# A hybrid decoder layer on one core: the mixer's input weights split early, stored in DRAM and read back as pairs

## The chip, the cores and the metric

The kernel runs on one core of a Trainium2 chip. The metric is the device time of one execution in microseconds (us): 1100.04 us is the median of 3 runs before the change (1100.03 to 1100.62). The engines are called as in the profile: PE (TensorE matmuls; PEld its weight loads), DVE (VectorE), ACT (ScalarE), POOL (GpSimd) and SP (SyncE, which here issues nearly all DMAs, in one queue).

## What is computed

One layer on 512 tokens of width 1024, in three sub-layers, each followed by a layer norm:

```python
mod = silu(c) @ w_ada + b_ada                 # 9 vectors of 1024: shifts, scales, gates
h = swiglu_ffn(modulate(x, sh1, sc1), w1, w3, w2);  x = layer_norm(ALPHA * x + 0.5 * g1 * h)
h = hybrid_mixer(modulate(x, sh2, sc2), w_in, ...); x = layer_norm(ALPHA * x + g2 * h)
h = swiglu_ffn(modulate(x, sh3, sc3), w1', w3', w2'); x = layer_norm(ALPHA * x + 0.5 * g3 * h)
```

The mixer multiplies its input by `w_in` (1024 x 3280), and from the columns come a sparse attention (index scores, top-k by repeated maximum, softmax over the kept keys) and a gated delta rule (short convolutions, a triangular inverse per chunk, a recurrence over four chunks). Both go through `w_out`.

## The kernel before, in words

**Split products.** Matmuls in fp32 are made of three matmuls in the faster fp32r type: every operand is split into a high part (a rounded copy, made by ACT) and a low part (the rest, made by a subtraction), and `mm3` issues high*high, high*low and low*high into one PSUM bank. A weight tile of 128 x 1024 takes one `wload` into a `raw` buffer, and `weights` turns it into `wh` and `wl` tiles, 512 columns at a time: `wh` by ACT, `wl` by DVE, or by POOL where the call says `pool=True`. There are 5 raw buffers (NRAW) and 86 tiles of 128 x 512 (NBIG), of which the weights' parts may hold a quota (`wf` 32, `wm` 16, `wb` and `w2` 28).

**Stages.** The first feed-forward network runs first: a first group of four hidden tiles (`first_group`, PSUM tiles `g`), then 18 steps f with 48 matmuls each (tiles `p`), then the down-projection in ten pieces (tiles `y`). In it, `ada` computes the modulation: 72 chunks of `w_ada`, each a load into a raw buffer and one multiply-and-sum on DVE (`raw<-raw,silu_c`); 16 stand ahead of the first matmuls, 2 follow each step f and 3 each piece of the down-projection until all are done.

The mixer's step `first` makes two key and value tiles and four index-query tiles from `wina` (8 blocks of 128 x 768, loaded into `wb` tiles and split by ACT and POOL). The other 20 column tiles come from `winb`: `project` loads one 128 x 1024 tile, splits it with ACT and POOL, and multiplies it in 24 matmuls (tiles `pj`). Steps `pk`, `pq`, `pv` convolve them, `qa` makes attention queries, `z` gates. `ix`, `tk`, `lg`, `av` are index scores, top-k, softmax weights and values (tiles `pt`, `pv`). `pre` and `sub` prepare and invert the triangular blocks: `sub` takes two raw buffers (`bl`, `Y`) and runs 31 pairs of a product and a subtraction on DVE, and then `m64`, `m128`, `rec` (one after the other over the four chunks) and `out` follow; they are the tail of the mixer, ahead of most of the output projection (tiles `y`), which again is split by ACT and DVE. The second network is built as the first.

**What sets the order.** Every operation is recorded first (so nearly all rows of the profile have line 561, that of the emitting loop), and a planner puts them in order: each has a priority by its place in the program, a table `ORDER` gives the mixer's steps and their delays, and the planner plays its own model of the engines, the buffers and the quotas. The result is a fixed order on every engine and in SP's queue. On the chip each engine keeps to it and waits at semaphores.

Of the kernel before, what the change touches and what calls it, by code (L numbers as in the profile page):

```python
# [11 lines left out]
F32 = mybir.dt.float32  # L12
F32R = mybir.dt.float32r
# [4 lines left out]
P = 128  # L18
T = 512
D = 1024  # L20
KD = D // P
# [5 lines left out]
NBIG, NRAW, WF, WM, WB, W2 = 86, 5, 32, 16, 28, 28  # L27
SKEW, DEFER = 3, 500
ALPHA = 2.0 ** 0.25
LN_EPS = 1e-5  # L30
# [534 lines left out]
class Build:  # L565
# [54 lines left out]
    def weights(s, src, n, pool=False, big=False):  # L620
# [22 lines left out]
        return get  # L643

    def mm3(s, out, wh, wl, xh, xl, start, stop):
        mm = s.nc.tensor.matmul
        mm(out, wh, xh, start=start, stop=False)
        mm(out, wh, xl, start=False, stop=False)
        mm(out, wl, xh, start=False, stop=stop)

    def setup(s):
        nc = s.nc
        s.par = s.keep(NPAR, "par")
        s.cst = s.keep(NCST, "cst")
        s.sc = s.keep(D, "silu_c")
        s.g.strict = True
        nc.sync.dma_start(s.sc, s.d["c"].broadcast_to([P, D]))
        nc.scalar.activation(s.sc, s.sc, AF.Silu)
        s.mod = {v: s.keep(8, f"mod_{v}") for v in range(9)}
        s.ada_next = 0  # L660
        s.early = [s.wload(s.d["wada"][j], D) for j in range(2)]
        nc.sync.dma_start(s.par, s.d["par"])
        zero, pb = s.t("zero")[:, 0:P], s.bank("warm")[:, 0:P]
        nc.gpsimd.memset(zero, 0.0)
        for _ in range(WARM):
            nc.tensor.matmul(pb, zero, zero, start=True, stop=True)
# [19 lines left out]
    def ada_some(s, n):  # L686
        for _ in range(n):
            if s.ada_next < len(ADA_CHUNKS):
                s.ada()

    def glu(s, p1, p3):
        nc = s.nc
# [4 lines left out]

    def first_group(s, src, us, halves, big=False):


        nb = src.shape[2] // P
        banks = [s.bank("g") for _ in range(nb)]
# [3 lines left out]
        def go(k, c0, c1):  # L706
            uh, ul = us(k, c0, c1)
            if k not in ws:
                q, s.quota = s.quota, "w2" if s.quota == "wm" else "wb"
                ws[k] = s.weights(src[k], nb * P, pool=True, big=True)  # L710
                s.quota = q
# [13 lines left out]
    def ffn(s, n, us, halves, ada_plan, res):  # L725
# [11 lines left out]
        for f in range(NF - G0[n]):  # L737
# [6 lines left out]
            hs.append(s.glu(p1, p3))  # L744
            s.ada_some(ada_plan(f))
        ws = {}
        for dt, c0, c1 in pieces(2):
# [9 lines left out]
            if c1 == T:  # L757
                del ws[dt]
            s.ada_some(ada_plan(100 + dt))

# [82 lines left out]
def body(s):  # L843
# [31 lines left out]

    s.ffn(1, us1, ALL, lambda f: 2 if f < 100 else 3, res1)

# [97 lines left out]

    s.ffn(2, u3, HALF, lambda f: 0, res3)
    fin = ln_apply(s.p_("ln3g"), s.p_("ln3b"), None, None, need_u=False)
# [86 lines left out]
def project(s, us, i, n=2):  # L1064

    res = []
    for b in range(n):
        w = s.weights(s.d["winb"][i + b], 1024, pool=True)
        pb = s.bank("pj")
# [121 lines left out]
def attend_values(s, ps, v2, qt, g, att):  # L1191
# [18 lines left out]
    for j in range(2):  # L1210
# [5 lines left out]

ORDER = ("first qi0 qa0:5766 ks:51 pk1:451 spill:57 pk3:1103 pq1:8 z2 qi1:17 gt:131 ix1 pv2:684 pq2:3860 pk2:1987 "
# [5 lines left out]

# [16 lines left out]
class Mixer:  # L1240
# [25 lines left out]
    def first(s):  # L1266

        b, nc = s.b, s.nc
        banks = b.first_group(b.d["wina"], s.us, HALF)
        b.quota = "wm"  # L1270
# [169 lines left out]
    def sub(s):  # L1440
# [3 lines left out]
        bl, Y = (b.g.tile(b.wraw, [P, B * B], F32, "raw", b.name(t), NRAW)[:n] for t in ("bl", "Y"))  # L1444
        tmp = b.sc[:n]
        for c in range(4):
# [167 lines left out]
```

## Time and profile before

| | |
|---|---|
| median of 3 runs | 1100.04 us |
| the profiled execution | 1099.98 us, span 1098.2 us |
| PE busy | 1061.3 us (97%) |
| DVE busy | 679.3 us (62%) |
| ACT busy | 414.9 us (38%) |
| POOL busy | 302.3 us (28%) |
| moved by DMA | 137.92 MB, mean 126 GB/s |

The span is what the profile covers; the execution's own time is 1.8 us longer. PE's busy time is a modelled one: matmuls overlap, so that a busy PE need not run at its peak, and a lower granted clock makes the same matmuls busy for longer. Shares over the span are means over very different stages; the rows ahead of the prediction are therefore by stage.

### The profile page before, as it was taken

To read this page: it belongs to the slowest core of one execution; us is meant where nothing else is said; L and a number is where in the kernel's file an instruction comes from. 1 tells how busy PE (TensorE), PEld (TensorE's weight loads), DVE (VectorE), ACT (ScalarE), POOL (GpSimd) and SP (SyncE) were. 2 spreads that over 40 slices of the span, in tenths; PEclk is the share of its full clock that TensorE was granted. 3 is DMA by queue.
4 is the path that set the end of the run, shared out by engine and by line. 5 is a ranking of instruction groups with operands and counts; after the bars stand their busy time and mean duration, and the time that the engine had idled before them with its cause. 6 is when DMAs were issued, how large, how long until landed. Compare 5 with 4: busy or idle time off the path is not lost.

```text
span 1098.2 us, 15160 instructions
## 1 busy us (share of the span) xinstructions
PE 1061.3 (97%) x5520; PEld 904.5 (82%) x5520; DVE 679.3 (62%) x1506; ACT 414.9 (38%) x866; POOL 302.3 (28%) x308
## 2 busy tenths in 40 slices
PE   8999999999999989999969999999999999999996
PEld 6788888888888988787747898989888888888896
DVE  7997655547672466999988999884333323333314
ACT  3353323233231434765832566443333322322203
POOL 4600000000222695496824311695000000002210
PEclk9999999999999999998959999999999999999998
DMA  9878555547642412131112303611323222243002
GB/s 359 314 278 316 206 179 196 172 138 244 221 156 91 137 54 98 40 109 46 44 43 52 103 21 125 235 45 41 113 83 110 92 81 72 68 144 106 16 1 77
DMA packets 52203, 137.92 MB, mean 126 GB/s; under 512 B 11360, under 2 KB 15584, under 8 KB 52128
## 3 DMA queue, kind: packets, MB, share of 16 engines
q1 hardware_dynamic: 52048, 136.69, 37.4%
q8 instruction: 43, 0.70, 0.3%
q14 instruction: 32, 0.26, 0.1%
q0 software_dynamic: 80, 0.26, 0.1%
HBM read 131.17 MB, written 5.77 MB: 125 GB/s over the span
## 4 chain that ended last, share of the span: by engine, by line
PE 75%; DVE 15%; issue 3%; ACT 3%; POOL 3%; DMA 1%; SPq 0%; POOLq 0%; ACTq 0%; DVEq 0%
PE p L561 37%; PE y L561 26%; PE g L561 6%; DVE sc L561 2%; DVE raw L561 2%; POOL wl L561 2%; DVE m L561 1%; PE pv L561 1%; DVE cv L561 1%; DVE x L561 1%; PE pj L561 1%; DVE u L561 1%; DVE Y L561 1%; PE pt L561 1%; DVE ptl L561 1%
## 5 line engine op out<-in xcount | busy, mean ns | idle before, releaser
L561 DVE TENSOR_TENSOR wl<-raw,wh 128x512 fp32r<-128x512 f32 (+1 forms) x260 | 180.1, 709 | 151.8 <-ACT wh L561 79.5
L561 ACT ACTIVATE wh<-raw 128x512 fp32r<-128x512 f32 (+1 forms) x300 | 174.7, 615 | 186.1 <-PE y L561 82.4
L561 PE MATMUL p<-ul,wh 128*128 128x512 f32 x592 | 230.3, 389 | 0.0
L561 PE MATMUL p<-uh,wh 128*128 128x512 f32 x592 | 230.3, 389 | 0.0
L561 PE MATMUL p<-uh,wl 128*128 128x512 f32 x592 | 230.3, 389 | 0.0
L561 PE MATMUL y<-hh,wl 128*128 128x512 f32 (+1 forms) x440 | 152.9, 347 | 0.0
L561 PE MATMUL y<-hl,wh 128*128 128x512 f32 (+1 forms) x440 | 152.7, 347 | 0.0
L561 PE MATMUL y<-hh,wh 128*128 128x512 f32 (+1 forms) x440 | 152.5, 347 | 0.0
L561 DVE CUSTOM_DVE_ANT_0 raw<-raw,silu_c 128x1024 f32<-128x1024 f32 x72 | 96.8, 1354 | 75.5 <-DMA raw<-in_wada_dram 75.5
L561 POOL TENSOR_SCALAR s<-x 128x512 f32<-128x512 f32 x3 | 4.0, 1332 | 461.4 <-DVE x L561 461.4
L561 PEld LDWEIGHTS p<-ul,wh 128*128 128x128 f32 x592 | 111.2, 188 | 23.2
L561 PEld LDWEIGHTS p<-uh,wl 128*128 128x128 f32 x592 | 111.1, 188 | 22.9
L561 PEld LDWEIGHTS p<-uh,wh 128*128 128x128 f32 x592 | 111.2, 188 | 22.8
L561 PEld LDWEIGHTS y<-hh,wh 128*128 128x128 f32 x440 | 83.3, 189 | 10.4
L561 PEld LDWEIGHTS y<-hl,wh 128*128 128x128 f32 x440 | 83.3, 189 | 10.4
L561 PEld LDWEIGHTS y<-hh,wl 128*128 128x128 f32 x440 | 83.3, 189 | 10.2
L561 ACT ACTIVATE hh<-sil 128x512 fp32r<-128x512 f32 x44 | 27.7, 633 | 154.9 <-DVE sil L561 135.0
L561 PE MATMUL g<-ul,wh 128*128 128x256 f32 (+1 forms) x256 | 78.8, 319 | 1.7 <-DVE ul L561 1.6
L561 PE MATMUL g<-uh,wh 128*128 128x256 f32 (+1 forms) x256 | 66.4, 316 | 9.9 <-ACT uh L561 9.9
L561 PE MATMUL g<-uh,wl 128*128 128x256 f32 (+1 forms) x256 | 75.5, 316 | 0.0
L561 POOL TENSOR_TENSOR wl<-wb,wh 128x512 fp32r<-128x512 f32 (+1 forms) x48 | 61.1, 1295 | 22.6 <-DMA wb<-in_f1a_dram 18.1
L561 POOL TENSOR_TENSOR s<-s,x 128x512 f32<-128x512 f32 (+1 forms) x21 | 28.5, 1356 | 137.0 <-DVE x L561 126.0
(254 smaller groups left out, 1826.8 us busy)
## 6 DMA issues: line engine op xcount, KB each, us to landing
raw<-in_wada_dram SPq DMA_DIRECT2D x72, 512.0 KB
raw<-in_f2b_dram SPq DMA_DIRECT2D x38, 512.0 KB
raw<-in_f1b_dram SPq DMA_DIRECT2D x36, 512.0 KB
raw<-in_winb_dram SPq DMA_DIRECT2D x20, 512.0 KB
raw<-in_f1c_dram SPq DMA_DIRECT2D x16, 512.0 KB
raw<-in_f2c_dram SPq DMA_DIRECT2D x16, 512.0 KB
wb<-in_f1a_dram SPq DMA_DIRECT2D x16, 256.0 KB
raw<-in_wout_dram SPq DMA_DIRECT2D x8, 512.0 KB
```

The source lines that it names most:

```text
L561: getattr(getattr(s.nc, o.eng), o.meth)(*[real(x) for x in o.args], **{k: real(v) for k, v in o.kw.items()})
```

## The change

A new step, `presplit`, runs beside the first network: once behind each of the 18 steps f and twice behind each piece of the down-projection, until the 8 tiles of `wina` and the 20 of `winb` are done. It loads a tile into a raw buffer, ACT writes the high part into a second raw buffer, DVE puts the low part in the place of the tile, and two DMAs write both to DRAM tensors (`dwa`, `dwb`). In the mixer, `stored` takes the place of `weights`: it reads the two parts back, those of `wina` into 512-column tiles (`wd`), those of `winb` into two raw buffers, from which the matmuls read. No engine splits these weights in the mixer. The modulation's chunks get other places: 3 behind each of the first four pieces only, and the last 8 behind the steps of the second network. `sub` takes a tile of its own for its products (`tmp`) in place of the buffer of silu(c), which is needed longer. The table `ORDER` is another one.

```diff
+    def presplit(s):
+        nc = s.nc
+        if s.pre_next >= KD + 20:
+            return
+        i, s.pre_next = s.pre_next, s.pre_next + 1
+        n, src = (768, s.d["wina"][i]) if i < KD else (1024, s.d["winb"][i - KD])
+        dst = s.dwa[i] if i < KD else s.dwb[i - KD]
+        raw = s.wload(src, n)
+        hi = s.g.tile(s.wraw, [P, 1024], F32, "raw", s.name("rawh"), NRAW)
+        nc.scalar.activation(hi[:, :n].bitcast(F32R), raw[:, :n], AF.Copy)
+        nc.vector.tensor_sub(raw[:, :n].bitcast(F32R), raw[:, :n], hi[:, :n])
+        nc.sync.dma_start(dst[0], hi[:, :n])
+        nc.sync.dma_start(dst[1], raw[:, :n])
+
+    def stored(s, src, n, big=False):
...
+            else:
+                x = s.g.tile(s.wraw, [P, 1024], F32, "raw", s.name("wd"), NRAW)
+                nc.sync.dma_start(x[:, :n], src[j])
+                parts.append([x[:, o:o + 512] for o in range(0, n, 512)])
...
+    def plan(s, f):
+        s.ada_some(2 if f < 100 else 3 if f < 104 else 0)
+        for _ in range(PRE_F if f < 100 else PRE_D):
+            s.presplit()
...
-    s.ffn(1, us1, ALL, lambda f: 2 if f < 100 else 3, res1)
+    s.ffn(1, us1, ALL, s.plan, res1)
-    s.ffn(2, u3, HALF, lambda f: 0, res3)
+    s.ffn(2, u3, HALF, lambda f: s.ada_some(1), res3)
-        w = s.weights(s.d["winb"][i + b], 1024, pool=True)
+        w = s.stored(s.dwb[i + b], 1024)
-        banks = b.first_group(b.d["wina"], s.us, HALF)
+        banks = b.first_group(b.dwa, s.us, HALF, nb=6)
-ORDER = ("first qi0 qa0:5766 ks:51 pk1:451 spill:57 pk3:1103 pq1:8 z2 qi1:17 gt:131 ix1 pv2:684 pq2:3860 pk2:1987 "
+ORDER = ("first qi0:239 ks:38 qa0:3221 pk2:3522 pv2:686 gt:451 pq2:815 z2:82 qi1:275 pk3:561 ix2 ix3:175 ix1 pk1 "
-        tmp = b.sc[:n]
+        tmp = b.t("tmp")[:n]
```

The first place is SP's queue beside the steps f of the first network. Before, two tiles of `f1b` (the network's own weights) and two of `wada` take turns:

```order
L561 DMA raw_1096<-in_f1b_dram 128x1024
L561 DMA raw_1119<-in_f1b_dram 128x1024
L561 DMA raw_1134<-in_wada_dram 128x1024
L561 DMA raw_1170<-in_wada_dram 128x1024
L561 DMA raw_1175<-in_f1b_dram 128x1024
L561 DMA raw_1205<-in_f1b_dram 128x1024
L561 DMA raw_1219<-in_wada_dram 128x1024
```

In the change, beside a later step:

```order
L562 DMA raw_1243<-in_winb_dram 128x1024
L562 DMA raw_1257<-in_f1b_dram 128x1024
L562 DMA raw_1272<-in_f1b_dram 128x1024
L562 DMA raw_1277<-in_wada_dram 128x1024
L562 DMA dwb<-rawh_1275 128x1024
L562 DMA dwb<-raw_1243 128x1024
L562 DMA raw_1319<-in_wada_dram 128x1024
L562 DMA raw_1334<-in_winb_dram 128x1024
```

A load of `winb` and two stores have come between the loads of each step, and the stores wait in the queue for ACT and DVE.

The second place is PE's order in the recurrence, between the second chunk's new state (`Sn`, `o`) and the products of the third chunk with it (`kS`, `qS`). Before, some fifty rows of attention stand between the two, of which these are the first:

```order
L561 MATMUL Sn_6105<-dl_6090,ktok_4604 128x128 x4
L561 MATMUL o_6115<-dl_6090,aq_5233 128x128 x4
L561 MATMUL pv_6124<-pth_6099,vh_4824 128x256
L561 MATMUL pv_6124<-ptl_6111,vh_4824 128x256
L561 MATMUL pv_6124<-pth_6099,vl_4835 128x256
L561 MATMUL pv_6124<-pth_6099,vh_4854 128x256
L561 MATMUL pv_6124<-ptl_6111,vh_4854 128x256
```

In the change:

```order
L562 MATMUL Sn_6429<-dl_6417,ktok_4605 128x128 x4
L562 MATMUL o_6439<-dl_6417,aq_5241 128x128 x4
L562 MATMUL y_1334_6448<-X_6272,y_1333_6431 128x128 x4
L562 MATMUL kS_6457<-S_6441,cv_4255 128x128
L562 MATMUL kS_6457<-S_6441,cv_4142 128x128
L562 MATMUL kS_6457<-S_6441,cv_4428 128x128
```

The attention work has left this stretch: between the first product of `m64` and the last transpose of `out`, 48 of 56 `pt`, 77 of 89 `pv` and all 32 `lg` matmuls now stand ahead of it.

The third place is DVE's order within `sub` (in the change its products go to `tmp`). Rope and query rows (`rq`, `rp`, `qs`) of the last attention queries, which before stood behind `sub`, now stand between its pairs:

```order
L562 TENSOR_TENSOR rp_5733<-rp_5733,sw_5730 128x512
L562 TENSOR_TENSOR Y_5100<-Y_5100,tmp_5558 64x15x17
L562 TENSOR_TENSOR atl_5394<-pv_5563,ath_5384 128x128
L562 TENSOR_TENSOR tmp_5558<-bl_5278,Y_5100 64x252
L562 TENSOR_TENSOR qs_5755<-rp_5733,qs_5755 64x512
L562 TENSOR_TENSOR Y_5100<-Y_5100,tmp_5558 64x14x18
L562 TENSOR_TENSOR qs_5761<-rp_5733,qs_5761 64x512
```

In all, DVE has 324 rows between the last `ul` ahead of the mixer and the first pair of `sub` (282 before), 132 from there to its last pair (103 before) and 222 (294 before) from there to the next norm's `ul`.

## Rows read from the trace of the kernel before

**Rows 1.** Windows by stage: window, then busy us (instructions) by engine, PEclk, DMA, GB/s

```profile
52.00:258.00 206.00, 206.00 (x909) 170.62 (x910) 135.66 (x258) 69.51 (x126) 0.43 (x1) 1.00 0.62 209
258.00:381.00 123.00, 123.00 (x676) 107.63 (x675) 65.40 (x134) 33.76 (x63) 34.92 (x31) 1.00 0.51 165
381.00:395.00 14.00, 11.58 (x96) 11.18 (x95) 10.17 (x22) 8.51 (x20) 12.93 (x14) 1.00 0.34 114
425.00:560.00 135.00, 126.56 (x593) 101.67 (x591) 126.70 (x329) 90.83 (x209) 89.62 (x89) 0.93 0.19 61
560.00:597.00 37.00, 31.56 (x134) 25.54 (x134) 32.96 (x104) 11.47 (x31) 9.48 (x12) 0.78 0.00 1
597.00:676.00 79.00, 77.56 (x570) 70.35 (x568) 70.65 (x258) 45.05 (x133) 18.46 (x23) 1.00 0.28 84
395.00:676.00 281.00, 265.23 (x1510) 225.56 (x1510) 244.79 (x714) 150.90 (x380) 143.48 (x158) 0.93 0.20 64
730.00:1098.00 368.00, 359.38 (x1821) 307.56 (x1820) 132.55 (x232) 108.59 (x195) 44.40 (x50) 0.99 0.24 75
```

**Rows 2.** The chain that ended last, first network: start us, us, what

```profile
62.06 195.84 PE p L561 x864
```

**Rows 3.** Groups of POOL, 381 to 700 us: busy us, mean ns, then idle before

```profile
L561 POOL TENSOR_TENSOR wl<-raw,wh 128x512 fp32r<-128x512 f32 x36 | 48.4, 1360 | 28.7 <-ACT wh L561 20.8 <-PE pj L561 7.9
L561 POOL TENSOR_TENSOR wl<-wb,wh 128x512 fp32r<-128x512 f32 (+1 forms) x14 | 14.7, 1077 | 1.0 <-ACT wh L561 0.9
```

**Rows 4.** Groups of DVE by form, 395 to 676 us

```profile
L561 DVE TENSOR_TENSOR qs<-rp,qs 64x512 fp32r<-64x512 f32 x16 | 14.5, 904 | 0.4
L561 DVE TENSOR_TENSOR ptl<-pt,pth 128x512 fp32r<-128x512 f32 x20 | 13.2, 686 | 3.2 <-ACT pth L561 3.1
...
L561 DVE SCALAR_TENSOR_TENSOR ul<-u,ln_B,uh 128x256 fp32r<-128x256 f32 x8 | 7.1, 927 | 0.0
...
L561 DVE SCALAR_TENSOR_TENSOR u<-x,ln_A,rows 128x256 f32<-128x256 f32 x6 | 2.7, 471 | 0.0
```

**Rows 5.** DVE in order of time, inside `sub`: start us, us, instruction

```profile
583.22 1.40 DVE L561 TENSOR_TENSOR silu_c<-bl,Y 64x255 f32<-64x255 f32 x1
584.65 0.42 DVE L561 TENSOR_TENSOR Y<-Y,silu_c 64x255 f32<-64x255 f32 x1
```

**Rows 6.** POOL in order of time, the same stretch

```profile
582.93 1.41 POOL L561 TENSOR_TENSOR wl<-raw,wh 128x512 fp32r<-128x512 f32 x1 [1.39 <-ACT wh L561]
```

**Rows 7.** Groups of DVE by form, 52 to 258 us

```profile
L561 DVE TENSOR_TENSOR wl<-raw,wh 128x512 fp32r<-128x512 f32 x83 | 55.9, 690 | 11.3 <-PE p L561 9.6 <-ACT wh L561 1.3
L561 DVE CUSTOM_DVE_ANT_0 raw<-raw,silu_c 128x1024 f32<-128x1024 f32 x42 | 51.0, 1224 | 51.4 <-DMA raw<-in_wada_dram 51.4
```

**Rows 8.** Windows in which the DMA engines were fullest (columns as in rows 1)

```profile
0.00:25.00 25.00, 20.08 (x95) 16.81 (x96) 17.23 (x27) 8.60 (x13) 10.38 (x12) 1.00 0.94 356
...
75.00:100.00 25.00, 25.00 (x112) 20.68 (x112) 23.65 (x48) 11.30 (x21) 0.00 (x0) 1.00 0.95 338
```

**Rows 9.** Waits of SP's queue, 52 to 258 us: us in total, times, longest

```profile
SPq L561 <- DVE mod L561: 125.9, 56, 5.8
```

**Rows 10.** The chain that ended last, 596 to 680 us: start us, us, what

```profile
606.79 0.60 DVE X L561
...
621.28 0.89 PE dl L561 x8
...
636.01 0.97 PE Sn L561 x8
...
644.09 0.89 PE kS L561 x8
...
654.25 1.03 DVE S L561 x4
...
656.23 1.12 DVE vr L561 x4
```

**Rows 11.** The store of `Y`, in SP's queue

```profile
596.66 0.50 SPq L561 DMA_DIRECT2D dX<-Y  x1
```

More of the change, by code (lines that the diff above doesn't have):

```diff
@@ L28 @@
 SKEW, DEFER = 3, 500
+PRE_F, PRE_D = 1, 2
 ALPHA = 2.0 ** 0.25
@@ L643, in weights, with get @@
         return get
+    def presplit(s):
[12 more added lines that the diff above has]
+    def stored(s, src, n, big=False):
+        nc = s.nc
+        parts = []
+        for j in range(2):
+            if big:
+                ts = []
+                for o in range(0, n, 512):
+                    m = min(512, n - o)
+                    q, s.g.quota = s.g.quota, s.quota
+                    x = s.t("wd")[:, :m]
+                    s.g.quota = q
+                    s.g.late = s.g.ahead
+                    nc.sync.dma_start(x, src[j][:, o:o + m])
+                    s.g.late = 0
+                    ts.append(x)
+                parts.append(ts)
+            else:
+                x = s.g.tile(s.wraw, [P, 1024], F32, "raw", s.name("wd"), NRAW)
+                nc.sync.dma_start(x[:, :n], src[j])
+                parts.append([x[:, o:o + 512] for o in range(0, n, 512)])
+        def get(i):
+            o = (i % 4) * P
+            return tuple(ts[i // 4][:, o:o + P].bitcast(F32R) for ts in parts)
+        return get
     def mm3(s, out, wh, wl, xh, xl, start, stop):
@@ L659, in setup @@
         s.mod = {v: s.keep(8, f"mod_{v}") for v in range(9)}
-        s.ada_next = 0
+        s.ada_next = s.pre_next = 0
+        s.dwa = s.g.tile(s.dram, [KD, 2, P, 768], F32, "dwa", "dwa")
+        s.dwb = s.g.tile(s.dram, [20, 2, P, 1024], F32, "dwb", "dwb")
         s.early = [s.wload(s.d["wada"][j], D) for j in range(2)]
@@ L696, in glu, with first_group @@
         return s.split(a, "h")
-    def first_group(s, src, us, halves, big=False):
-        nb = src.shape[2] // P
+    def first_group(s, src, us, halves, big=False, nb=None):
+        nb = nb or src.shape[2] // P
         banks = [s.bank("g") for _ in range(nb)]
@@ L709, in go @@
                 q, s.quota = s.quota, "w2" if s.quota == "wm" else "wb"
-                ws[k] = s.weights(src[k], nb * P, pool=True, big=True)
+                if len(src.shape) == 4:
+                    ws[k] = s.stored(src[k], nb * P, big=True)
+                else:
+                    ws[k] = s.weights(src[k], nb * P, pool=True, big=True)
                 s.quota = q
@@ L744, in ffn @@
             hs.append(s.glu(p1, p3))
-            s.ada_some(ada_plan(f))
+            ada_plan(f)
         ws = {}
@@ L758, in ffn @@
                 del ws[dt]
-            s.ada_some(ada_plan(100 + dt))
+            ada_plan(100 + dt)
     def rsqrt(s, v, w, n=3):
```

10 rows, old and new, of the table ORDER are left out of this document.

## Prediction

> **What bounds the kernel now.** I read first the windows by stage, then the chain that ended last, then the groups of POOL and DVE inside the mixer, and last SP's queue and the DMA windows. The reader is to see three things.
>
> In the first network PE has no gap: 206.00 busy of 206 us and 123.00 of 123 us [rows 1], 864 matmuls in 195.84 us or 0.227 us each [rows 2]. Whatever is added there can be hidden or can hurt; it cannot gain. The same holds for the second network.
>
> In the mixer, from 395 to 676 us, PE is busy 265.23 of 281 us, so 15.8 us are idle, and its granted clock is 0.93 [rows 1]: part of the stretch was at 1.2 in place of 2.4 GHz, behind idle stretches, and a mean of 0.93 costs at most 0.07 x 281 = 19.7 us of work at half speed. About 35 us is all that this stage can give back.
>
> DVE is what PE waits for there: busy 126.70 of 135 us up to 560, 32.96 of 37 in the inversion `sub`, 70.65 of 79 in the tail [rows 1]. PE is granted only 0.78 beside `sub`. So the change pays if it makes DVE's work shorter or lets something else run beside it.
>
> **What leaves the mixer.** 40 half tiles of `winb` and 16 pieces of `wina` lose their split. On POOL the rows show 36 splits of 1.360 us and 14 of 1.077 us up to 700 us, 63 us together [rows 3]; on ACT as many copies. Neither engine bounds the stage (POOL is busy 143.48 of 281 us, ACT 150.90 [rows 1]), so their time itself is worth nothing. DVE loses no instruction. What it loses is a neighbour. Inside `sub` a product that takes about 0.42 us took 1.40 us [rows 5] while POOL ran a split of 1.41 us [rows 6]: 0.98 us lost. The `qs` subtractions take 904 ns, where `ptl`, the same operation as long, takes 686; `ul` takes 927 ns and `u`, as long, 471 [rows 4]. That is 16 x 0.218 + 8 x 0.456 = 7.1 us on 24 instructions. Bounds: nothing, if POOL's other work meets the same DVE instructions instead; 0.98 us for half of the 50 splits, 25 us. I take 10 us, near what the two groups show, for all of DVE's forms.
>
> The Trainium skill ("SBUF — State Buffer", on engine port contention) calls this an exclusive lock: a DVE instruction with two SBUF inputs and a POOL instruction that reads SBUF do not overlap at all. The pair of rows agrees. By that rule all 50 splits could each give back their whole meeting, which is the third rival below.
>
> **What moves within the mixer.** The order of the change shows where DVE's work goes. One DVE row of this stage takes 244.79 / 714 = 0.343 us [rows 1]; with that:
>
> - Up to the first pair of `sub`: 324 rows in place of 282, so 42 x 0.343 = 14.4 us more, less 10 us of lost neighbour, less 1 us that falls into DVE's 8.3 idle us: +3 us. The 2 to 3 weight tiles that fit the raw buffers are enough here, since PE has room.
> - Inside `sub`: 132 in place of 103, 29 x 0.343 = 9.9 us more, of which about 3 fill the 4.0 idle us and 1 is the blocked product: +6 us.
> - The tail, 597 to 676 us, loses 294 - 222 = 72 rows or 24.7 us of DVE's work, and on PE 48 `pt`, 77 `pv` and 32 `lg` matmuls. What is left is a chain. From the store of `Y` at 596.66 [rows 11] to the first product with it at 606.79 and to the first `dl` at 621.28 it took 10 and 14.5 us [rows 10]; I leave these nearly as they are (9 and 14.5). From there to the last `vr` at 656.23 it took 35 us for three further chunks. Bare, one chunk is kS 0.89, vr 1.12, dl 0.89, its copy about 0.6 (an estimate by ACT's neighbours), Sn 0.97, S 1.03 [rows 10], 5.5 us, and I add 0.2 us for each of five hand-overs: 6.5 us, 19.5 for three, and 4 for the first. With 9 for `out` in place of some 14 (less beside it on DVE) the tail is 9 + 14.5 + 4 + 19.5 + 9 = 56 us in place of 79: -23 us. Its ends: -12, if hand-overs are twice as many and half of the gain in `out` stays away, and -28.
>
> The mixer: 3 + 6 - 23 = -14 us, with ends of about -30 and +2 when the ends of DVE's relief are put in. Check against PE: -14 leaves 21 of the 35 us that PE can give, so PE does not become the bound.
>
> Ahead of it, between 381 and 395 us, PE is idle 2.4 of 14 us while POOL is busy 12.93 [rows 1]; splits of `wina` go, DVE's `ul` come sooner: -1 us (0 to -2).
>
> **What the first network takes over.** 28 tiles: ACT copies, DVE subtractions and three DMAs each. DVE: at most two lengths of 690 ns [rows 7] each, 28 x 1.38 = 39 us, against 206 - 135.66 + 123 - 65.40 = 128 idle us [rows 1]. ACT has more room. Both cost nothing while weights are ahead of PE. Of the modulation, 8 chunks of 1.224 us [rows 7] go to the second network, where DVE is busy 132.55 of 368 us [rows 1]: nothing.
>
> The DMAs are the tight part. A step f moved 4 x 0.524 = 2.1 MB in 48 x 0.227 = 10.9 us; with `wina` it moves 3.3 MB (300 GB/s) and with `winb` 3.7 MB (337 GB/s). One piece of the down-projection (66 matmuls, 15.0 us) goes from 3.0 to 6.2 MB, 411 GB/s, for four pieces. The fullest windows show 356 GB/s at a share of 0.94 and 338 at 0.95 [rows 8]. But the weights run ahead. Adding up SP's queue, 87.0 MB stand there up to the first tile of the fifth piece; from about 45 us at 356 GB/s that is at 45 + 244 = 289 us, and PE needs the tile at 62 + 196 + 4 x 15.0 = 318 us, or some 8 us earlier with landing and split. So 21 us are in hand, and the queue must keep up 87.0 / 265 = 328 GB/s. It is no longer free for that: SP's waits were already 125.9 us for raw buffers [rows 9], and the stores add waits for ACT and DVE ahead of the network's own loads. No row shows a store of this size among such loads. Bounds: 0, and 25 us at 300 GB/s (290 us for the 87.0 MB, 25 over). I take 2 us.
>
> **The sum.** 1099.98 (the profiled execution, 0.06 under the median of the runs) + 2 - 1 - 14 = 1087 us.
>
> **Rivals.**
>
> *The first network starves* (slower). In SP's one queue a store that waits for DVE holds the network's loads behind it, five raw buffers are shared by two more users, and the DMAs are nearly full. For it: the 92% that the queue must hold for 265 us, which the trace shows for 25 us at a time; against it: 21 us in hand. The point is the rate: below 328 GB/s PE waits, at 87.0 / 279 = 312 GB/s the wait is 14 us and eats the gain, at 300 it is 25 us: 1099.98 + 25 - 15 = 1110 us. The Trainium skill ("DMA: Bandwidth & Descriptors", anatomy of one DMA) puts most of a DMA's fixed 2 us on the write receipt, heaviest in HBM, which speaks for this rival: 56 stores would hold raw buffers for 112 us more, an estimate by that page, 22 us for each of the five. No row shows it, and nothing above uses it.
>
> *The raw buffers bind in the mixer.* Before, a projection's weights waited in 4 tiles apart from the raw buffers; now a pair holds two of five buffers until its 24 matmuls are done, and `sub` holds two more. Beside `sub` one pair is left; each of the last four projections then waits for its loads, 1.05 MB or 2.9 us at 356 GB/s and about as long again to land. With 10 us lost of 15: 1097 us, on the edge of no change.
>
> *DVE's neighbour was worth more.* The 25 us end of the relief in place of 10, and what PE's low clock took comes back too: 1099.98 - 30 = 1070 us.
>
> **How the numbers follow.** The forecast gets 0.52 (its own range 1080 to 1095), the raw buffers 0.17, the starved network 0.17, the larger relief 0.14. About 0.2% (2.2 us) can be told from no change. Faster: the forecast, the larger relief, and a little over half of the raw-buffer case, 0.75. Same: 0.07, most of it from that case and from a starved network that just eats the gain. Slower: 0.18. The range goes down to 1070 and up to 1105, which leaves out the worst of the starved cases and what lies beyond the larger relief.
>
> **What would show it.** Right: PE without gaps up to about 381 us; `qs` and `ul` near 690 and 480 ns; the mixer's dense output projection beginning some 14 us earlier, the rows from `Y`'s store to it shortened by over 20 us while those ahead of `sub` are no shorter; DMA share near 0.9 from 60 to 300 us. Wrong: `p` or `y` matmuls that wait for `raw` tiles of `f1b` or `f1c`, the clock low beside them (the starved network); `pj` weight loads that wait for `dwb` (raw buffers); a tail as long as before, which would mean that its length was the chain and not what stood in it.

## The result, and the profile after

| | before | after |
|---|---|---|
| median of 4 runs each | 1100.03 us | 1083.53 us (1080.6 to 1085.25) |
| ratio, with its 95% interval | | 0.9848 (0.9822 to 0.9874) |
| profiled execution, its span | 1099.98, 1098.2 us | 1082.16, 1080.4 us |
| moved by DMA | 137.92 MB | 192.45 MB |
| POOL busy | 302.3 us | 236.6 us |

The change is 16.5 us faster; the prediction was 1087.0 us in a range from 1070 to 1105. The sum of its terms can be compared piece by piece. The stages are read from the rows in order of time: the end of the down-projection's last `y` matmul, the start of the first `pj`, the start of the first subtraction of `sub` on DVE and the end of its last, the last `y` of the mixer's output projection, the end. All in us:

| stage | before | after | difference | predicted |
|---|---|---|---|---|
| first network, to its last `y` | 381.2 | 388.4 | +7.2 | +2 |
| norm and first group, to the first `pj` | 43.1 | 40.7 | -2.4 | -1 |
| to the first pair of `sub` | 135.6 | 134.0 | -1.6 | +3 |
| `sub` | 36.7 | 38.8 | +2.1 | +6 |
| from `sub` to the end of the output projection | 118.3 | 91.8 | -26.5 | -23 |
| norm and second network | 383.3 | 386.7 | +3.4 | 0 |
| span | 1098.2 | 1080.4 | -17.8 | -13 |

The windows by stage of the changed kernel, with the columns of [rows 1]; the stages begin and end some us later than before:

```profile
52.00:258.00 206.00, 206.00 (x910) 170.54 (x910) 150.45 (x261) 85.43 (x138) 0.16 (x1) 1.00 0.90 320
258.00:388.00 130.00, 124.39 (x673) 108.16 (x672) 74.36 (x134) 40.38 (x69) 27.58 (x29) 0.97 0.78 277
388.40:402.20 13.80, 12.43 (x105) 12.23 (x104) 8.63 (x22) 2.76 (x7) 8.94 (x14) 1.00 0.34 113
425.00:563.00 138.00, 135.71 (x698) 111.10 (x696) 135.44 (x377) 92.81 (x213) 59.23 (x71) 1.00 0.36 122
563.00:602.00 39.00, 37.06 (x200) 31.02 (x199) 37.16 (x136) 16.19 (x44) 6.34 (x11) 1.00 0.38 132
602.00:660.00 58.00, 56.56 (x442) 53.41 (x440) 50.13 (x188) 30.28 (x92) 8.22 (x9) 1.00 0.36 101
395.00:660.00 265.00, 257.97 (x1571) 223.97 (x1570) 233.62 (x722) 143.55 (x356) 85.77 (x108) 1.00 0.35 113
712.00:1080.00 368.00, 359.20 (x1827) 307.59 (x1826) 141.70 (x257) 107.47 (x192) 43.03 (x43) 0.99 0.27 86
```

Three things are to be seen. From 395 us to the last transpose of `out` the mixer holds 722 DVE rows, about as many as before (714), in 265 us in place of 281, and PE's granted clock there is 1.00 in place of 0.93. (The first network ends 6.6 us ahead of 395 us here and 13.8 us ahead of it before, so counted from its end the stretch is 23 us shorter.) POOL has lost 50 rows and 58 us. And in the down-projection PE is no longer without gaps: 124.39 busy of 130 us, at a mean clock of 0.97.

DVE's groups by form, 395 to 676 us, which answer to [rows 4]:

```profile
L562 DVE TENSOR_TENSOR ptl<-pt,pth 128x512 fp32r<-128x512 f32 x20 | 12.9, 678 | 0.3 <-ACT pth L562 0.3
L562 DVE TENSOR_TENSOR qs<-rp,qs 64x512 fp32r<-64x512 f32 x16 | 11.0, 690 | 0.5
...
L562 DVE SCALAR_TENSOR_TENSOR ul<-u,ln_B,uh 128x256 fp32r<-128x256 f32 x8 | 4.9, 626 | 0.7 <-ACT uh L562 0.6
...
```

`qs` has come down from 904 to 690 ns, near the 678 of `ptl`; `ul` from 927 to 626, still above `u` (470).

The chain that ended last, 596 to 720 us (start us, us, what), beside [rows 10]:

```profile
623.05 0.89 PE dl L562 x8
...
632.43 0.89 PE dl L562 x8
...
639.12 0.45 PE dl L562 x4
...
645.36 0.23 PE dl L562 x2
...
689.55 0.69 PE st L562 x8
...
694.23 1.23 POOL wl L562
695.46 0.86 POOL m L562
```

The first `dl` comes 21.1 us after the store of `Y` (601.95 us), 24.6 before. The further chunks follow at 9.4, 6.7 and 6.2 us (12.6, 14.0 and 9.2 before). The last rows belong to the stage that was predicted to lose nothing: the norm's operation on POOL (`m`) starts 5.2 us after the end of the norm's sums (`st`), behind a split of the second network's weights.

**Where the first network lost its 7 us.** SP's queue, 290 to 325 us (start us, us, issues):

```profile
295.65 2.40 SPq L562 DMA_DIRECT2D raw<-in_f1c_dram  x2
...
303.49 3.60 SPq L562 DMA_DIRECT2D raw<-in_winb_dram  x2
309.62 7.99 SPq L562 DMA_DIRECT2D dwb<-rawh  x2
318.19 0.33 SPq L562 DMA_DIRECT2D raw<-in_f1c_dram  x1
```

Two stores of high parts stood at the head of the queue for 8 us, and the load that PE needs, `f1c`, behind them. The second store waited 7.3 us for ACT's copy, and ACT shows why that was late:

```profile
316.19 1.06 ACT L562 ACTIVATE rawh<-raw 128x1024 fp32r<-128x1024 f32 x1 [3.12 <-DVE mod L562]
```

It waited for DVE to finish a chunk of the modulation and leave a raw buffer. And DVE was late, since the angles of the rotary embedding are made just there, and two of its rows took long:

```profile
312.13 1.80 DVE L562 SCALAR_TENSOR_TENSOR sin<-n,sin 128x512 f32<-128x512 f32 x1
313.85 2.30 DVE L562 CUSTOM_DVE_ANT_0 raw<-raw,silu_c 128x1024 f32<-128x1024 f32 x1
```

against 0.68 for the row of `sin` ahead of it and 1.21 for the chunk behind. Both are rows with two SBUF inputs, and POOL ran two such rows at just that time:

```profile
312.03 1.34 POOL L562 TENSOR_TENSOR s<-s,x 128x512 f32<-128x512 f32 x1 [11.67 <-DVE x L562]
313.33 1.73 POOL L562 TENSOR_TENSOR s<-s,sq 128x512 f32<-128x512 f32 x1
```

It is the same pairing as in the mixer before the change, and each of the two rows is 1.1 us longer here than its neighbour. The windows show what the hold-up did to the DMA engines, and the third row the mean over the 265 us of the prediction's sum:

```profile
258.00:300.00 42.00, 42.00 (x187) 34.79 (x186) 23.94 (x40) 13.69 (x21) 4.79 (x6) 1.00 0.94 348
300.00:323.00 23.00, 17.45 (x77) 14.11 (x76) 18.35 (x31) 6.50 (x11) 4.87 (x4) 0.93 0.64 234
...
45.00:310.00 265.00, 264.56 (x1166) 218.47 (x1166) 189.18 (x328) 105.22 (x169) 11.98 (x12) 1.00 0.89 321
```

From 258 to 300 us the rate is 348 GB/s, more than the 328 that the sum asked for. Then it falls to 234 at a share of 0.64, while loads stand in the queue: PE waits 5.6 us, and with a granted clock of 0.93 over 23 us it loses up to another 1.6. But the rate had not been enough before either: 320 GB/s from 52 to 258 us and 321 over the sum's 265 us, 85.1 of the 87.0 MB, which is 6 us short at 328. In all this time SP waited for raw buffers and for the data of stores, 160 us in total from 52 to 258. So PE starved for bytes that came a little late, and the last of the delay was made by one queue, in its order, over five raw buffers.

### The profile page after: what moved, and what is told of

It is laid out like the page before. It is cut to its first block, busy times and chain, and to the rows that moved or that the text cites. A ratio compares the mean times of both kernels' runs of the same rounds, so it can differ in the third digit from the quotient of the medians.

```text
span 1080.4 us, 15261 instructions
## 1 busy us (share of the span) xinstructions
PE 1047.3 (97%) x5520; PEld 896.9 (83%) x5520; DVE 694.8 (64%) x1534; ACT 422.3 (39%) x842; POOL 236.6 (22%) x252
## 2 busy tenths in 40 slices
DMA packets 69484, 192.45 MB, mean 178 GB/s; under 512 B 13281, under 2 KB 18529, under 8 KB 69409
## 4 chain that ended last, share of the span: by engine, by line
PE 54%; DVE 17%; DMA 16%; issue 8%; ACT 3%; POOL 1%; SPq 0%; ACTq 0%; DVEq 0%; POOLq 0%
PE y L562 22%; PE p L562 19%; PE g L562 5%; DMA raw<-in_winb_dram 5%; DVE raw L562 4%; PE pj L562 3%; DVE wl L562 3%; DMA raw<-in_f1c_dram 3%; DMA raw<-in_f1b_dram 2%; DVE sc L562 2%; DVE m L562 2%; DMA dwb<-rawh 1%; ACT rawh L562 1%; DMA raw<-in_wada_dram 1%; DMA raw<-in_wina_dram 1%
## 5 line engine op out<-in xcount | busy, mean ns | idle before, releaser
L562 DVE TENSOR_TENSOR wl<-raw,wh 128x512 fp32r<-128x512 f32 (+1 forms) x260 | 173.6, 692 | 153.2 <-ACT wh L562 100.0
L562 ACT ACTIVATE wh<-raw 128x512 fp32r<-128x512 f32 (+1 forms) x260 | 149.6, 611 | 127.6 <-PE y L562 47.1
L562 DVE CUSTOM_DVE_ANT_0 raw<-raw,silu_c 128x1024 f32<-128x1024 f32 x72 | 100.0, 1392 | 39.8 <-DMA raw<-in_wada_dram 39.0
L562 PE MATMUL pj<-uh,wd 128*128 128x512 f32 x320 | 103.6, 395 | 1.0 <-DMA wd<-dwb 0.9
L562 PEld LDWEIGHTS pj<-uh,wd 128*128 128x128 f32 x320 | 59.6, 188 | 13.0 <-DMA wd<-dwb 1.5
L562 ACT ACTIVATE rawh<-raw 128x1024 fp32r<-128x1024 f32 (+1 forms) x28 | 28.0, 1001 | 107.3 <-DMA raw<-in_winb_dram 81.7
L562 PE MATMUL pj<-ul,wd 128*128 128x512 f32 x160 | 63.0, 394 | 0.0
```

Source lines behind the costliest of these rows:

```text
L562: getattr(getattr(s.nc, o.eng), o.meth)(*[real(x) for x in o.args], **{k: real(v) for k, v in o.kw.items()})
```

## The experiments

Each edit is planned anew as a whole, so the runs are compared by stage (us, in the order of the table above; the first two rows repeat it).

| kernel | first network | to `pj` | to `sub` | `sub` | to the end of the output projection | rest |
|---|---|---|---|---|---|---|
| before | 381.2 | 43.1 | 135.6 | 36.7 | 118.3 | 383.3 |
| after | 388.4 | 40.7 | 134.0 | 38.8 | 91.8 | 386.7 |
| e_spread | 381.8 | 40.7 | 134.0 | 38.5 | 91.6 | 387.4 |
| e_nohi | 381.2 | 40.7 | 134.0 | 38.4 | 92.9 | 386.1 |
| e_actq | 401.5 | 40.7 | 134.0 | 38.4 | 92.4 | 386.6 |
| e_hit | 389.3 | 40.7 | 134.0 | 39.1 | 91.2 | 387.5 |
| e_poolback | 384.5 | 43.2 | 141.8 | 51.3 | 93.1 | 387.8 |
| e_poolset | 389.2 | 40.0 | 157.1 | 41.9 | 94.5 | 390.5 |
| b_neworder | 381.3 | 43.4 | 164.0 | 22.7 | 156.1 | 382.4 |
| s_oldorder | 381.1 | 39.9 | 142.4 | 33.9 | 133.9 | 391.5 |
| s_adalate | 381.3 | 40.7 | 134.0 | 38.3 | 92.3 | 390.6 |
| s_f2dve | 381.0 | 40.7 | 134.0 | 38.4 | 92.0 | 384.9 |

In the four runs on the first network, and in the two on the second, the mixer's stages repeat within about 1 us: what they show of the stage that was edited can be read alone.

### The first network: bytes, queue or buffers

**e_spread**

```diff
-PRE_F, PRE_D = 1, 2
+PRE_F, PRE_D = 1, 1
```

> One pre-split behind each piece of the down-projection in place of two (PRE_D = 1), so that the same 28 tiles are spread over all ten pieces. In the changed kernel PE waits 5.6 us for the weights of the fifth piece and the first network ends at 388.4 us in place of 381.2. Theory 1, the DMA engines were asked for more than they moved (328 GB/s needed by the sum, 320 measured): pieces one to four now carry some 4.6 MB each (about 305 GB/s) in place of 6.2, the wait shrinks to 2 us or less, the network ends at 382 to 384 us and the time is about 1078 us. Rival, the wait was already made among the steps f, by raw buffers and by stores in the queue, and the pieces only showed it: the wait stays at 4 us or more, 1082 to 1084 us. Third possibility: the last pair of winb is stored later and the mixer waits for it, no gain or a loss in spite of a shorter first network.

Measured: 1075.79 us, 0.9781 of the kernel before (0.9766 to 0.9795); the first network ends at 381.8 us. The windows of this kernel beside the two above:

```profile
258.00:300.00 42.00, 41.58 (x183) 34.11 (x183) 29.96 (x54) 14.65 (x26) 2.20 (x3) 1.00 0.93 342
300.00:323.00 23.00, 23.00 (x103) 19.03 (x102) 14.14 (x15) 9.66 (x17) 9.69 (x7) 1.00 0.82 293
```

The whole loss is gone, and nothing is paid for it later. The time alone does not tell bytes from queue, since the edit takes from both: the loads and stores of four tiles leave the sum's stretch, and the rate is no higher here (342 GB/s in the first 42 us, where the change has 348).

**e_nohi**

```diff
-        nc.sync.dma_start(dst[0], hi[:, :n])
...
-                nc.sync.dma_start(x[:, :n], src[j])
+                nc.sync.dma_start(x[:, :n], src[1])
```

> The high parts are not stored, and the mixer reads the low parts twice in their place: the values of the mixer's projections are left wrong by this, the instructions and the loads in the mixer stay. 28 stores, 13.6 MB, leave the first network; loads, splits and raw buffers stay. Theory 1 (bytes): up to the first tile of the fifth piece there are about 75 MB in place of 87, which needs 283 GB/s; the wait of 5.6 us goes, the first network ends at 381 to 382 us, about 1076 us. Rival (the queue: the loads stand behind stores that wait for ACT and DVE): SP still waits for DVE's low part with every one of the other 28 stores, so at least half of the wait stays, the first network ends at 384 us or later, 1079 us or more.

Measured: 1074.96 us, first network to 381.2 us. This kernel leaves out the stores of the high parts. The time is as the theory of the bytes said; but the stores that went are also those that stood at the head of the queue above, so this run, too, fits both.

**e_actq**

```diff
-        nc.sync.dma_start(dst[0], hi[:, :n])
-        nc.sync.dma_start(dst[1], raw[:, :n])
+        nc.scalar.dma_start(dst[0], hi[:, :n])
+        nc.scalar.dma_start(dst[1], raw[:, :n])
```

> Both stores of each pre-split are issued on ACT's own DMA queue in place of SP's. The bytes are the same. In SP's queue the stores waited 27.7 us for ACT and 14.4 us for DVE between 52 and 258 us, with the network's loads behind them. Theory 1 (bytes): the mean from 52 to 258 us stays near 320 GB/s, the wait for the fifth piece stays at 4 to 7 us, 1082 to 1085 us. Rival (the queue): with nothing ahead of the loads the mean rises to 330 GB/s or more, the wait shrinks to 2 us or less, the first network ends at 381 to 384 us, about 1077 us.

Measured: 1092.91 us, the first network to 401.5 us: both theories missed, and on the far side. Waits of SP's queue, 52 to 258 us (us in total, times, longest):

```profile
SPq L562 <- DMA dwb<-rawh: 56.4, 9, 7.0
...
SPq L562 <- DMA dwa<-rawh: 43.1, 7, 6.6
```

With the stores in another queue the loads meet the same raw buffers from the other side: a load into a buffer that held a high part now waits for the store to land, 99.5 us in all (14.0 in the change), and the mean rate from 52 to 258 us falls from 320 to 300 GB/s. Where an operation waits was moved; that five buffers carry four users was not.

**e_hit**

```diff
-        hi = s.g.tile(s.wraw, [P, 1024], F32, "raw", s.name("rawh"), NRAW)
-        nc.scalar.activation(hi[:, :n].bitcast(F32R), raw[:, :n], AF.Copy)
-        nc.vector.tensor_sub(raw[:, :n].bitcast(F32R), raw[:, :n], hi[:, :n])
-        nc.sync.dma_start(dst[0], hi[:, :n])
+        for o in range(0, n, 512):
+            m = min(512, n - o)
+            hi = s.t("th")[:, :m]
+            nc.scalar.activation(hi.bitcast(F32R), raw[:, o:o + m], AF.Copy)
+            nc.vector.tensor_sub(raw[:, o:o + m].bitcast(F32R), raw[:, o:o + m], hi)
+            nc.sync.dma_start(dst[0][:, o:o + m], hi)
```

> The changed kernel (two pre-splits behind each piece), but the high part goes into 512-column tiles of the big pool in place of a second raw buffer; it is stored in halves. The bytes are the same; a pre-split now holds one of the five raw buffers in place of two. Issued on ACT's queue the stores made things worse (first network to 401.5 us): SP's loads then waited 99 us for high parts to land in DRAM, so a buffer that holds a high part may be what is short. Theory of the buffers: the loads run ahead, more than 325 GB/s from 52 to 258 us, the wait for the fifth piece shrinks to 2 us or less, first network to 381 to 384 us, time 1075 to 1078 us. Rival (bytes): the rate stays near 320 GB/s and the network ends at 386 to 390 us, 1081 to 1086 us.

Measured: 1083.46 us, the network to 389.3 us; no gain. Its windows, and behind them those of the change:

```profile
75.00:165.00 90.00, 90.00 (x399) 74.53 (x398) 71.98 (x136) 41.63 (x75) 0.00 (x0) 1.00 1.00 374
165.00:258.00 93.00, 93.00 (x412) 77.02 (x411) 51.38 (x94) 31.50 (x57) 0.00 (x0) 1.00 0.70 239
258.00:318.00 60.00, 57.12 (x244) 46.38 (x243) 43.64 (x80) 20.34 (x38) 14.36 (x7) 0.97 0.99 364
```

```profile
75.00:165.00 90.00, 90.00 (x399) 74.53 (x398) 64.26 (x113) 35.30 (x58) 0.00 (x0) 1.00 0.93 332
165.00:258.00 93.00, 93.00 (x412) 77.02 (x411) 66.14 (x113) 38.45 (x61) 0.00 (x0) 1.00 0.91 327
258.00:318.00 60.00, 59.45 (x263) 48.89 (x261) 39.73 (x67) 19.57 (x30) 9.66 (x9) 1.00 0.82 306
```

This run shows what the engines can move. With one raw buffer less per pre-split they reach 374 GB/s at a share of 1.00 for 90 us, stores among loads: the 332 of the change was not their limit. The buffers are the nearest cause, though the edit also cuts one store in two. But running ahead ends somewhere: from 165 us on only 239 GB/s are asked for, with idle DMA engines, and at the pieces, which ask for 411, even 364 is too little. Which limit stopped the running ahead (the quota of 32 tiles for the network's weights is the nearest) was not tried.

### The mixer: POOL's splits, or the order

**e_poolback**

```diff
+        if not big:
+            for o in range(2):
+                lo = s.t("pw")
+                nc.gpsimd.tensor_sub(lo, parts[0][o], parts[1][o])
```

> The changed kernel, and for each half tile of winb that the mixer reads back one POOL subtraction of 128x512 more (high minus low part into a tile that nobody uses), as POOL had before: 40 in place of the 36 to 40 removed, 1.36 us each. DMAs and DVE's instructions stay those of the change. Theory of the lost neighbour: qs goes back from 690 to about 900 ns and ul from 626 to about 900, the mixer is about 10 us longer and the time near 1093 us. Rival, the gain of the mixer is the order alone (attention work out of the tail): the time stays within 3 us of 1083.5. If it is much more than 10 us, the neighbour was worth more than the 10 us of the sum and the order less.

Measured: 1110.17 us median, 1103.45 in the profiled execution, which is 21 us above that of the change. Up to `sub` +7.8 us, inside it +12.5, behind it +1.3. The other three runs are 6 to 9 us slower than the profiled one and have no trace. The windows from the first network's end to the end of `sub`, of the change and of this kernel:

```profile
388.30:601.90 213.60, 208.01 (x1188) 177.16 (x1187) 188.18 (x548) 114.50 (x268) 83.62 (x108) 1.00 0.35 121
```

```profile
384.40:620.80 236.40, 218.45 (x1207) 184.25 (x1206) 205.64 (x555) 117.88 (x277) 137.34 (x150) 0.97 0.30 107
```

DVE needs 205.64 us for 555 rows in place of 188.18 for 548: 0.371 against 0.343 us a row, or 15 us over the 548. The rows of the forms that both kernels have equally often there, 498 of them, are 15.3 us longer in all. By form (DVE, 395 to 676 us):

```profile
L562 DVE TENSOR_TENSOR qs<-rp,qs 64x512 fp32r<-64x512 f32 x16 | 14.0, 874 | 0.7 <-ACT qs L562 0.2
...
L562 DVE TENSOR_TENSOR tmp<-bl,Y 64x256 f32<-64x256 f32 x1 | 1.3, 1299 | 0.0
```

`qs` is back near its 904 ns, and rows of `sub` take 1.2 to 1.3 us where the change has 0.4. So POOL's subtractions cost DVE's rows 15 us. That the time of the run is longer by as much and more does not price the neighbour: in POOL's queue the added subtractions waited 44.9 us for pairs from DRAM, and POOL's own work stood behind them.

**e_poolset**

```diff
+        if not big:
+            for o in range(2):
+                lo = s.t("pw")
+                for _ in range(3):
+                    nc.gpsimd.memset(lo, 0.0)
```

> The changed kernel, and for each half tile of winb three POOL memsets of 128x512 into a tile that nobody uses (some 0.5 us each by the trace's memset of 64x1024 in 0.95 us) in place of the POOL subtraction that made it 1110 us. POOL is as busy as with the subtractions, but reads nothing. Theory of the neighbour (DVE loses time beside a POOL instruction that reads SBUF): qs stays near 690 ns, the mixer near 305 us, the time 1082 to 1088 us. Rival (POOL's own time: convolutions and softmax wait for POOL, which is late): 1097 us or more.

Measured: 1113.21 us, 1.0128 of before (1.0092 to 1.0163): the time lies in the rival's range, the rows that the run was made for are as the theory said. `qs` takes 707 ns, and `sub` 41.9 us in place of 51.3. Only 2 of the 16 `qs` met a memset, so the rows are better taken one by one: 20 `tensor_tensor` rows of DVE with two SBUF inputs ran for at least half their time beside the memsets, 7.9 us in all, where their forms take 8.6 in the change (by the median); 12 such rows beside the subtractions of e_poolback took 13.4 us in place of 4.8, and 5 with an input from PSUM 2.9 as in the change. So DVE rows with two SBUF inputs lose nothing beside a POOL instruction that only writes. But up to `sub` the run loses 23 us, and 9.0 us of DVE's time go in one row. DVE, then POOL, in order of time:

```profile
458.09 9.47 DVE L562 TENSOR_SCALAR sc<-rl,wi 128x512 f32<-128x512 f32 x1
```

```profile
458.80 8.48 POOL L562 MEMSET pw<- 128x512 f32 x18
```

The same row takes 0.47 us in the change; here it ends with the last of 18 memsets in a row. The Trainium skill ("SBUF — State Buffer", on who interferes with whom) draws this very line: a DVE instruction with two SBUF inputs meets only POOL instructions that read, a `tensor_scalar` in its two-port mode meets all of them. Both halves agree with this run. The rest of the 23 us (a second such row took 1.81 us, the other rows stand in another order) stays open. Up to the end of `sub` this run loses 26 us to e_poolback's 20, so that POOL's own lateness is not excluded as a part of e_poolback's loss.

**e_neworder and e_oldorder.** These were to swap the tables `ORDER` of the two kernels. The edits did not reach the table, so both kernels are unchanged: they are the kernel before and the change once more.

> The kernel before with the change's table ORDER and nothing else: the splits of the mixer's weights stay on ACT and POOL, nothing is stored. Theory A (the order only moves DVE's work out of the tail; what pays is the relief from POOL's splits): from the end of sub to the end of the output projection about 92 to 97 us in place of 118, the stretch ahead of it longer by about as much, 1096 to 1104 us in all. Rival B (the order is the gain): the tail is shorter and the front no longer, 1080 to 1090 us.

> The changed kernel with the table ORDER of before: the mixer's weights come as stored pairs, the attention work stays in the tail. Theory A (the relief pays): DVE gets back 15 to 20 us in the mixer, so from the end of the first network to the end of the output projection 313 to 320 us in place of 333.8 before and 305.3 in the change, with a tail of 105 us or more; the time is 1090 to 1098 us, the 7 us of the first network included. Rival B (the order is the gain): 328 us or more, 1103 us or more.

Measured: 1099.22 us (1.0004 of before, 0.9995 to 1.0013) and 1081.99 us (0.9842, 0.9827 to 0.9857). They tell only how well a kernel repeats, and nothing of the theories.

**b_neworder and s_oldorder.** The swap itself, the second on top of e_spread:

```diff
-ORDER = ("first qi0 qa0:5766 ks:51 pk1:451 spill:57 pk3:1103 pq1:8 z2 qi1:17 gt:131 ix1 pv2:684 pq2:3860 pk2:1987 "
+ORDER = ("first qi0:239 ks:38 qa0:3221 pk2:3522 pv2:686 gt:451 pq2:815 z2:82 qi1:275 pk3:561 ix2 ix3:175 ix1 pk1 "
```

> The kernel before with the change's table ORDER (this time the table that orders the mixer's steps) and nothing else: the mixer's weights are split there by ACT and POOL as before. Theory A (the order only moves DVE's work, what pays is the relief from POOL's splits): the stretch from sub's end to the end of the output projection gets shorter than 118 us, the one ahead of it longer by about as much, and the time stays between 1092 and 1105 us. Rival B (the order is the gain): 1090 us or less.

> Stored pairs, one pre-split behind each piece (1075.8 us in its run), with the table ORDER of before: 44 of the 80 transposes of attention weights stand behind the first product of m64 again, 8 in the change. Theory A (relief pays, the order only moves): from the end of the first network to the end of the output projection within 5 us of 305, 1071 to 1081 us, with a long tail and a shorter front. Rival B (the order is needed for the gain, since the tail is a chain in which DVE's work is in the way): 315 us or more there, 1086 us or more.

Measured: 1151.03 us (1.0462) and 1124.24 us (1.0218, against 0.9781 with the change's own table). The first lies outside both of its theories. The second meets rival B's words (1086 us or more), but so far above them that the lost gain alone, 24 us, does not explain it. The windows of b_neworder around `sub`:

```profile
589.00:611.00 22.00, 0.00 (x0) 0.00 (x0) 20.02 (x59) 0.00 (x0) 0.00 (x0) 0.50 0.07 28
611.00:767.00 156.00, 141.51 (x886) 123.64 (x887) 110.30 (x348) 70.71 (x194) 47.29 (x48) 0.94 0.31 100
```

`sub` runs alone there, 22 us in which PE does nothing and its granted clock is 0.50, the lower of its two levels (1.2 GHz), and all that could have run beside it stands behind. A table of delays is made for one set of durations and places; with the splits in place of the pairs, or the other way round, it can put work where it meets nothing, as here (for s_oldorder that is argued, not shown). So the gain in time cannot be divided into one for the order and one for the splits: each table loses some 50 us with the other kernel.

The length of DVE's rows can be divided. From the first network's end to that of the output projection, over the rows of the forms that a kernel has as often as the change, some 730 to 750: the kernel before takes 14.2 us more than the change, b_neworder 17.5 more, s_oldorder 1.0 more. With either table the rows are long where POOL splits, and short where it does not.

### The norm ahead of the second network

**s_adalate** (on top of e_spread)

```diff
-    s.ffn(2, u3, HALF, lambda f: s.ada_some(1), res3)
+    s.ffn(2, u3, HALF, lambda f: s.ada_some(1 if f >= 8 else 0), res3)
```

> One pre-split behind each piece (as in the run before, 1075.8 us), and the last 8 chunks of the modulation behind the steps 8 to 15 of the second network in place of its steps 0 to 7. In the change PE stands 6 us between the output projection and the second network's first group, 0.5 us before; the norm's POOL operation waits there behind two splits of the network's first weights, whose loads came late behind a chunk's. Theory: without the chunks the weights come earlier, 3 to 4 us of the 6 go, 1072 to 1073 us. Rival (the planner's order of splits and norm makes it, whatever is loaded): the 6 us stay, 1075 to 1077 us.

Measured: 1077.72 us, the last stage 390.6 us in place of 387.4: not better but worse, so having the chunks there was not the cause. POOL, in order of time:

```profile
685.19 6.49 POOL L562 TENSOR_TENSOR wl<-wb,wh 128x512 fp32r<-128x512 f32 x5
691.64 0.70 POOL L562 TENSOR_TENSOR m<-m,cst 128x2 f32<-128x2 f32 x1
```

The norm's `m` comes behind five splits now, behind two in e_spread and the change, and behind none before:

```profile
711.38 0.71 POOL L561 TENSOR_TENSOR m<-m,cst 128x2 f32<-128x2 f32 x1 [3.15 <-DVE m L561]
```

**s_f2dve** (on top of e_spread)

```diff
-                    ws[k] = s.weights(src[k], nb * P, pool=True, big=True)
+                    ws[k] = s.weights(src[k], nb * P, pool=s.quota == "wb", big=True)
```

> One pre-split behind each piece (1075.8 us), and the splits of the second network's first weights go from POOL to DVE (16 of them, 128x512 and 128x256; 0.69 us for the longer in place of 1.2 on POOL). Taking the modulation's chunks away from this place had made the wait longer (10 us between the output projection and the first group, 6.3 with the chunks), and there the norm's one POOL operation (the power of -1/2) stood behind a run of splits on POOL. Theory (POOL's splits ahead of the norm make the wait): 3 to 5 us of the 6.3 go, 1071 to 1073 us. Rival (DVE, which now has the splits as well as the norm's other rows, is late instead): 5 us or more stay, 1075 us or more.

Measured: 1073.14 us, 0.9758 of before (0.9745 to 0.9772), the last stage 384.9 us in place of 387.4. Waits of PE, 676 to 700 us, of e_spread and of this kernel:

```profile
PE rows L562 <- POOL m L562: 2.6, 1, 2.6
PE rows L562 <- DVE m L562: 1.3, 1, 1.3
```

```profile
PE rows L562 <- DVE m L562: 1.7, 1, 1.7
PE rows L562 <- POOL m L562: 1.1, 1, 1.1
```

The time is just above the range of the theory and below that of the rival: POOL's splits made 1.5 us of this wait, and DVE, with the splits, gives 0.4 back. That is 1.1 of the 2.5 us; the rest lies further back in the network, in parts of less than 1 us, and was not followed. It is the fastest kernel of this study, 26.7 us under the kernel before.

## Why the prediction held, and where it did not

That the total was so near is in part luck, since errors cancel: three terms of the mixer were too dark by 4.6, 3.9 and 3.5 us, that of the first group by 1.4, and two terms outside too bright by 5.2 and 3.4. (The ends given for the mixer, -30 and +2, are not the sums of the ends of its terms, -34 and +7; the measured -26.0 lies inside either.)

**The tail** held, and in its mechanism. Predicted were 56 us up to the last transposes of `out`; they took 57.5 (601.9 to 659.4), where the kernel before took 79.9. Two errors cancel in it: the first `dl` came 21.1 us after the store in place of 23.5, and the advance per chunk, put at 6.5 us, came to 9.4, 6.7 and 6.2, a mean of 7.4. The 3.5 us more came behind it: the output projection needs 34.3 us from there in place of 38.4, as some of its matmuls fill the tail's gaps.

**DVE's neighbour** is the term that was mis-sized: "I take 10 us, near what the two groups show, for all of DVE's forms". The two groups behaved (`qs` 690 ns as said, `ul` only 626 in place of 480), but they were not the whole. Other forms became shorter too; one of them, before and then in the change (DVE, 395 to 676 us):

```profile
L561 DVE SCALAR_TENSOR_TENSOR sc<-rl,wi,sc 128x512 f32<-128x512 f32 x7 | 7.7, 1096 | 0.0
...
L562 DVE SCALAR_TENSOR_TENSOR sc<-rl,wi,sc 128x512 f32<-128x512 f32 x7 | 5.2, 738 | 0.0
```

Summed form by form up to the end of the output projection, DVE's rows of the kernel before are 20 us longer than at the change's lengths: 11.5 us of it ahead of `sub`, 3.1 in it, 5.3 behind. That is the relief, twice the 10 us; e_poolback, which puts POOL's subtractions back, makes DVE's rows some 15 us longer again. Of the 8.5 us by which the change is better than the sum up to the end of `sub`, it explains less than half, as 11 were counted there. More came from DVE's idle time ahead of `sub`: the sum let 1 of 8.3 us be filled, and it went from 8.3 us of 135 to 2.6 of 138 [rows 1 and the windows above]. The upper end, 25 us, was the better guide; the third rival's price was right in kind, but the first network took part of it away.

**The first network** is the step that failed. That "the queue must keep up 87.0 / 265 = 328 GB/s" was the right sum, and the queue kept up 321. The price of 2 us, with 21 us in hand, came from the 356 GB/s of the fullest windows, but SP's queue is in order and the buffers are five: its waits held the rate below what the engines can move (374 in e_hit), and at the end one copy that was late held two stores, and these the load, for 8 us. The starved rival had this mechanism ("a store that waits for DVE holds the network's loads behind it"), the right place and the right rule, and its sign was seen, a `y` matmul that waits for `f1c` with the clock low beside it; it only took the rate too low, 300 to 312 GB/s for 14 to 25 us. At 321 its own rule gives 6 us, and 7.2 were lost. How much of that belongs to the mean rate and how much to the 8 us at the queue's head stays open. e_spread shows that it was needless.

**The first group** gained 2.4 us in place of 1. PE's idle 2.4 us at its start became 1.4 of 13.8 (388.4 to 402.2 us), which is the 1 us of the sum; behind that the granted clock was 1.00, where before it was 0.94 from 395 to 425 us, up to 1.8 us.

**The second network** was to pay nothing for eight chunks on an engine with room. It did not pay for having the chunks at its start (s_adalate). It paid 3.4 us at its start, where the norm's one small row on POOL came to stand behind splits: PE waits 3.9 us there, 2.6 of them for that row, and its granted clock over the first 25 us of the stage is 0.86, where before it was 1.00. s_f2dve, without the splits on POOL, takes 2.5 of the loss away.

**The raw buffers in the mixer** did not bind: `pj` waited 0.9 us for `dwb`, while SP's queue stood 143 us waiting for `pj` to leave buffers, which cost nobody anything. PE's granted clock was 1.00 there; the 0.07 of before are part of the gain, as the check against PE's 35 us allowed.

## What to carry to other kernels

A transfer that is hidden on average is priced at the place where the queue is tightest: look for what stands at the head of an in-order queue there, what its data waits for, and how many buffers its users share, and take the rate that such a queue holds, not that of the fullest window. Engine time that costs nothing by itself can still cost its neighbour, and the few most conspicuous groups understate it: sum the lengthening over all rows of the engine that bounds the stage. And a table of delays belongs to the durations it was made with; neither half of such a change can be judged with the other half's table.

## What the hardware showed that was not expected

- A DVE `tensor_scalar` of 0.47 us took 9.47 us beside 18 POOL memsets in a row, and ended with the last of them.
- With stores among the loads the DMA engines moved 374 GB/s at a share of 1.00 for 90 us (e_hit), more than the 356 in the fullest window before [rows 8]. The Trainium skill ("Perfetto Trace Analysis", on engine utilization) says that a core alone can pass the 358 GB/s of its share; this run agrees.
- Stores of 512 KB took 5.6, 6.6 and 3.9 us from issue to landing in the chain of the change (`dwb<-rawh`, at 206.82, 227.66 and 253.84 us), no more than the loads around them, 3.5 to 6.9 us. The estimate of 2 us more for each, which the prediction gave beside the starved rival, finds no support in these three.
